# A hybrid decoder step: the bonus term taken out of the token stream, the inversion loading its own matrices, squared keys in another buffer, and the projection jobs in another order

## The chip, the core and the metric

One core of a Trainium2 chip runs the whole step in one launch. The metric is the device time of one execution in microseconds (us), as the median of three runs. Engines are named as in the profile: PE (matmul), DVE (vector), ACT (scalar), POOL (GpSimd), SP (the queue that issues most DMAs).

## The reference, cut to what matters

1024 prompt tokens and 8 x 8 sample tokens (1088 columns) go through one layer. A short convolution makes one half of the mixed vector, an RWKV-7 head group (8 heads of 64) the other; then come the output projection, a squared-ReLU MLP with 4096 hidden features, and the last RMSNorm.

```python
proj = h @ w_in
c_b, c_c, c_x, p_rw = jnp.split(proj, ...)
y_conv = c_b * short_conv(c_c * c_x)
xm = p_rw + (prev - p_rw) * mu
r, k, v, pw, pa, pg = jnp.split(xm, ...)
kk = k * k_k;  kk = kk / max(sqrt(sum(kk * kk)), 1e-12)
k = k * (1 + (a - 1) * k_a)
for t:                      # per head, S is 64 x 64
    S = S * w_t - (S kk_t) (kk_t * a_t)^T + v_t k_t^T
    y_t = S r_t
y = groupnorm(y)
bonus = sum(r * k * r_k, axis=-1, keepdims=True) * v
y_rwkv = (y + bonus) * g
x = x + concat([y_conv, y_rwkv]) @ w_out
x = x + square(relu(rmsnorm(x) @ w_ff1)) @ w_ff2
```

## The kernel before, in words

All matmuls on activations are done in three passes of split 32-bit numbers (high x high, high x low, low x high), 24 matmuls per 128 output features and token group. Tokens stand in three groups of 384, 384 and 320 columns.

**The delta rule in chunks.** The RWKV half is cut into 12 units `UN`: four head pairs p, three token groups g each, so unit u = 3p + g. A unit has six chunks of 64 tokens (five for g = 2, where the fifth holds the sample tokens). For each unit these steps follow each other:

- `gen_norms`: squared keys (ACT, L802), their sums per head (PE `pn`, L806), reciprocals (DVE, L810 to L814).
- `gen_ew`: decays, the modified key `kp`, the products `KB` and `AR`; then the Gram products `pm` (PE, L894), masked by DVE into `LT`, `AMB`, `AMK`. `LT` goes to DRAM and back as blocks of 32 x 32: SP writes `lt_d` (L920) and reads it into `M`, four partition copies inside the tile `gM` (L929). `M` is a single buffer.
- `gen_invert`: POOL inverts the 24 blocks of the unit by 31 pairs of instructions on `W` and `M` (L1024, L1026); SP then writes `w_d` (L1032).
- `gen_merge`: SP reads `Tt` (L1050), PE joins the block inverses (`pz`, L1058 and L1066).
- `gen_tokens`: transposed values `ptv` and keys `ptk` (PE), copied by ACT; after them, in the same stream, the bonus: `kp` times r and r_k (DVE, L969), its split (L973, L976), head sums `pb` (PE, L980), and `bv` (DVE, L986). At L969 the buffers of r and k, and at L986 that of v, are handed back.
- `gen_recur`: the serial recurrence over the chunks (`rc`, L1094 to L1110) and the outputs `py` (L1128); `gen_sample` for the sample chunk; `gen_finish`: GroupNorm (with one power on POOL, L1265), bonus, gate.

**What sets the order.** `Weave.run` takes all these generators, and the stream `fill` of projection matmuls (`acc`, L660), and writes out one fixed order for every engine. Each step names its engine, a planned cost and what must stand before it (`deps`, and credits of buffers in `acq`). A generator is strictly serial: a step that cannot be placed holds all later steps of that generator. On the chip each engine then runs its list in order. There are 24 projection jobs of 72 matmuls in the table `main`, at most two accumulators open. The r, k and v of one p come into three buffers each (`XB`), one per group, so the r projection of the next p needs a buffer that L969 has handed back.

Two waits of the planner matter here. In `gen_ew` the load of `M` for unit u comes as a step of that generator behind the mark `("inv", u - 1)`, the end of the inversion before, and only after it the mark `("A", u)` is set. In `gen_tokens` the bonus of unit u has `deps=[("A", u)]`:

```python
yield ck("SP", 1.6, nb=True, deps=[("inv", u - 1)] if u else [])
M = at["M"]
for i in range(4):
    SP.dma_start(M[24 * i:24 * i + nb], lt_d[:nb])
e["M"] = M
wv.mark(("A", u))
```

Behind the units come the output projection (`out_jobs`, L667), two FF1 jobs inside the weave, and from some 750 us on the MLP, which the change does not touch.

Of the kernel before, what the change touches and what calls it, by code (L numbers as in the profile page):

```python
# [28 lines left out]
REC, TR = 2, 2  # L29
# [4 lines left out]
def tile_kernel(ctx: ExitStack, tc: tile.TileContext, io: dict):  # L34
# [698 lines left out]
    main = (rkv_jobs(0) + conv_jobs(0, "cxb") + conv_jobs(1, "c") + rkv_jobs(1) + conv_jobs(1, "xb") + rkv_jobs(2)  # L733
# [60 lines left out]
    def gen_norms(u):  # L794
# [4 lines left out]
        yield ck("ACT", 0.5, deps=[("xk", p, g)] + ([("pb", u - 1)] if u else []))  # L799
        xk = xs["k", p, g]  # L800
        k2 = at["pe"].tile([128, 384], F32, tag="kx", name="k2")
# [5 lines left out]
        yield ck("DVE", 0.65)  # L807
# [13 lines left out]
    def gen_ew(u):  # L821
# [26 lines left out]
        yield ck("DVE", 0.99, deps=[("xk", p, g)] + ([("pb", u - 2)] if u > 1 else []))  # L848
        xk = xs["k", p, g]
        kp = at["pe"].tile([128, 384], F32, tag="kp", name="kp", bufs=2)  # L850
        e["kp"] = kp
# [74 lines left out]
        yield ck("SP", 1.6, nb=True, deps=[("inv", u - 1)] if u else [])  # L926
        M = at["M"]
        for i in range(4):
            SP.dma_start(M[24 * i:24 * i + nb], lt_d[:nb])  # L929
        e["M"] = M  # L930
        wv.mark(("A", u))
        wv.mark(("M", u), wv.now + 2.3)

    def gen_tokens(u):
# [18 lines left out]
        KT = at["KTs"][u % 2].rearrange("p c (x k) -> p c x k", x=2)  # L953
        for c0 in range(0, nch, 3):
            cc = range(c0, min(c0 + 3, nch))
            yield ck("PE", 0.108 * len(cc), acq=("tr",), deps=[("KB", u)] + done(u - 2))
            KB, kp = e["KB"], e["kp"]
            pt = ps.tile([128, 4, 128], F32, tag="tr", name="ptk", bufs=TR)
            for c in cc:
                PE.transpose(pt[:, c - c0, :], KB[:, c, :], ident)  # L960
            for h in range(2):
                for x in range(2):
                    yield ck("ACT", 0.35, lat=0)
                    A.copy(KT[HS[h], c0:cc[-1] + 1, x, HS[h]], pt[HS[x], 0:len(cc), HS[h]])
            wv.free("tr")
        yield ck("DVE", 0.5, deps=[("A", u)])
        wv.mark(("ptk", u))
        xr, xk = xs.pop(("r", p, g)), xs.pop(("k", p, g))
        V.scalar_tensor_tensor(kp[:, :n], xr[:, :n], vec("rk", p), kp[:, :n], op0=ALU.mult, op1=ALU.mult)  # L969
        wv.free("xr", "xk")  # L970
        yield ck("ACT", 0.42)
        rk_hi = at["pe"].tile([128, 384], F32R, tag="kx", name="rk_hi")
        A.copy(rk_hi[:, :n], kp[:, :n])  # L973
        yield ck("DVE", 0.5)
        rk_lo = at["pe"].tile([128, 384], F32R, tag="rkl", name="rk_lo")
        V.tensor_tensor(rk_lo[:, :n], kp[:, :n], rk_hi[:, :n].bitcast(F32), op=ALU.subtract)  # L976
        wv.mark(("rkr", u))
        yield ck("PE", 0.35, acq=("tr",), deps=[("F", u - 2)] if u > 1 else [])
        pb = ps.tile([128, 512], F32, tag="tr", name="pb", bufs=TR)
        PE.matmul(pb[:, :n], bonesr, rk_hi[:, :n], start=True, stop=False)  # L980
        PE.matmul(pb[:, :n], bonesr, rk_lo[:, :n], start=False, stop=True)
        wv.mark(("pb", u))
        yield ck("DVE", 0.5)
        xs.pop(("v", p, g))
        bv = at["pp"].tile([128, 384], F32, tag="bv", name="bv", bufs=2)
        V.tensor_tensor(bv[:, :n], pb[:, :n], xv[:, :n], op=ALU.mult)  # L986
        wv.free("tr", "xv")
        e.update(KT=KT, VT=VT, bv=bv)
# [13 lines left out]
    def gen_invert(u):  # L1002
# [5 lines left out]
        if u == 0:  # L1008
            yield ck("SP", 0.45)
            load_W(0)  # L1010
        W = Ws.pop(u)
        tmp = at["pp"].tile([96, 80], F32, tag="wtmp", name="wtmp")
        for r in range(31):
            if r == 0:
                yield ck("POOL", 0.63, lat=0, deps=[("M", u), ("W", u)])
                M = e["M"]
# [225 lines left out]
    def gen_finish(u):  # L1242
# [5 lines left out]
        yield ck("DVE", 0.7, deps=[("C", u)] + ([("Y", p)] if g == 2 else []))  # L1248
# [62 lines left out]
    def gen_rows():  # L1311

        for tag, k in ROWS:
            yield ck("ACT", 0.05, lat=0, acq=(tag,), deps=[("T", 10), ("mixd", 6), ("convd", 2, 0)])
            load_row(pa.tile([128, 384], F32, tag=tag, name="mr", bufs=XB[tag[1]]), 0, k)
        yield ck("NO", 0, deps=[("T", 11), ("rows", 0), ("row3", 2)])
# [129 lines left out]
    with tc.manual_schedule():  # L1446
# [13 lines left out]
        for t in range(3):  # L1460
# [6 lines left out]
            if t == 1:  # L1467
# [20 lines left out]
                chain(gen_tokens),  # L1488
# [177 lines left out]
```

## Time and profile before

| what | us |
|---|---|
| median of three runs | 1524.59 (1522.58 to 1525.06) |
| the profiled execution | 1522.59 |
| its span, first to last instruction | 1520.8 |
| PE busy | 1461.6 (96%) |
| DVE busy | 826.0 (54%) |
| POOL busy | 315.4 (21%) |

The page's strip of 40 slices gives the busy share of each engine in tenths, and PEclk the granted TensorE clock in tenths of full speed. A row of the windows view names a stretch, its length, the busy time of PE, PEld, DVE, ACT and POOL with instruction counts, the granted clock and the DMA share. In a timeline row the start, the duration, the engine, the line and the instruction stand, with the idle time before it in brackets. SPq rows are DMA issues.

### The profile page before, as it was taken

How to read it: one execution, taken by the hardware profiler on the slowest of the kernel's cores; microseconds unless marked ns; L12 is line 12 of the kernel's file. 1: busy time of each engine (PE TensorE's matmuls, PEld its weight loads, DVE VectorE, ACT ScalarE, POOL GpSimd, SP SyncE). 2: the span in 40 equal slices, each digit the busy share in tenths (PEclk: the TensorE clock that was granted, in tenths of full speed). 3: DMA queues.
4: the chain of work that ended last, by engine and by line, in shares of the span. 5: the costliest groups of instructions: out<-in, count | busy, mean ns of one | idle time of the engine just before them, and what ended most of it. 6: DMA issues, size and time to landing. Idle time of an engine off the chain costs nothing.

```text
span 1520.8 us, 25883 instructions
## 1 busy us (share of the span) xinstructions
PE 1461.6 (96%) x10163; PEld 1370.2 (90%) x10163; DVE 826.0 (54%) x1788; ACT 510.1 (34%) x1094; POOL 315.4 (21%) x855
## 2 busy tenths in 40 slices
PE   7999989979989998899999999999999999999997
PEld 5999879979978898799999999999999999999996
DVE  7538647956756866476633443434444444444447
ACT  6532234232423323344432222332223322233225
POOL 3022762573664656000000000000000000000004
PEclk9999969989978999699999999999999999999998
DMA  5243212311321241663321111111101111111103
GB/s 186 97 161 92 61 30 71 92 51 45 83 64 42 66 112 24 206 193 111 102 73 42 50 38 39 56 49 49 42 28 56 54 45 42 28 56 56 35 1 118
DMA packets 140228, 108.25 MB, mean 71 GB/s; under 512 B 43837, under 2 KB 131017, under 8 KB 140106
## 3 DMA queue, kind: packets, MB, share of 16 engines
q1 hardware_dynamic: 65322, 61.29, 13.5%
q10 hardware_dynamic: 74784, 45.30, 10.1%
q8 instruction: 80, 1.31, 0.4%
q14 instruction: 42, 0.34, 0.1%
HBM read 88.46 MB, written 18.09 MB: 70 GB/s over the span
## 4 chain that ended last, share of the span: by engine, by line
PE 77%; POOL 9%; DMA 4%; DVE 4%; issue 3%; SPq 1%; ACT 1%; POOLq 0%; ACTq 0%; DVEq 0%
PE acc L103 23%; PE acc L1531 16%; PE acc L660 13%; PE acc L1543 7%; PE acc L667 6%; POOL W L1026 4%; POOL wtmp L1024 4%; DMA wraw<-in_w_out 1%; PE py L1128 1%; PE pm L894 1%; PE pw L512 1%; DMA gM<-lt_d 1%; PE rc L1106 1%; PE rc L1110 1%; PE rc L1098 1%
## 5 line engine op out<-in xcount | busy, mean ns | idle before, releaser
L103 PE MATMUL acc<-h_lo,whi 128*128 128x320 f32 (+1 forms) x720 | 234.8, 326 | 0.0
L103 PE MATMUL acc<-h_hi,wlo 128*128 128x320 f32 (+1 forms) x720 | 234.8, 326 | 0.0
L103 PE MATMUL acc<-h_hi,whi 128*128 128x320 f32 (+1 forms) x720 | 234.7, 326 | 0.0
L660 PE MATMUL acc<-h_lo,whi 128*128 128x384 f32 (+1 forms) x672 | 229.5, 342 | 1.6 <-DVE h_lo L410 1.6
L660 PE MATMUL acc<-h_hi,whi 128*128 128x384 f32 (+1 forms) x672 | 229.7, 342 | 0.4 <-DVE nsT L259 0.3
L660 PE MATMUL acc<-h_hi,wlo 128*128 128x384 f32 (+1 forms) x672 | 229.3, 341 | 0.0
L1533 DVE TENSOR_TENSOR x<-acc,x 128x512 f32<-128x512 f32 (+1 forms) x193 | 132.7, 688 | 125.0 <-PE acc L1531 125.0
L1409 DVE TENSOR_TENSOR slo<-r,shi 128x384 fp32r<-128x384 f32 (+1 forms) x96 | 51.5, 536 | 204.5 <-ACT shi L1407 204.5
L1577 POOL TENSOR_TENSOR rsf<-rsf,nhalf 128x1 f32<-128x1 f32 (+1 forms) x9 | 8.0, 889 | 741.5 <-DVE rsf L1574 740.4
L1024 POOL TENSOR_TENSOR wtmp<-W,gM 96x60 f32<-96x60 f32 (+24 forms) x372 | 122.9, 330 | 160.5 <-DMA gM<-lt_d 83.4
L1531 PE MATMUL acc<-f2h,shi 128*128 128x512 f32 (+1 forms) x386 | 150.2, 389 | 0.0
L1531 PE MATMUL acc<-f2h,slo 128*128 128x512 f32 (+1 forms) x386 | 150.0, 389 | 0.0
L1531 PE MATMUL acc<-f2l,shi 128*128 128x512 f32 (+1 forms) x386 | 149.9, 388 | 0.0
L68 ACT CAST f2h<-f2r 128x1024 fp32r<-128x1024 f32 x32 | 32.0, 1046 | 309.1 <-PE acc L1531 309.1
L103 PEld LDWEIGHTS acc<-h_lo,whi 128*128 128x128 f32 x720 | 135.1, 188 | 0.6
L103 PEld LDWEIGHTS acc<-h_hi,whi 128*128 128x128 f32 x720 | 135.1, 188 | 0.6
L103 PEld LDWEIGHTS acc<-h_hi,wlo 128*128 128x128 f32 x720 | 135.2, 188 | 0.0
L660 PEld LDWEIGHTS acc<-h_lo,whi 128*128 128x128 f32 x672 | 129.1, 192 | 2.9 <-DVE h_lo L410 1.9
L660 PEld LDWEIGHTS acc<-h_hi,whi 128*128 128x128 f32 x672 | 129.4, 193 | 2.0 <-issue 0.4
L1026 POOL TENSOR_TENSOR W<-W,wtmp 96x60 f32<-96x60 f32 (+24 forms) x372 | 124.5, 335 | 29.1
L660 PEld LDWEIGHTS acc<-h_hi,wlo 128*128 128x128 f32 x672 | 129.3, 192 | 1.1
L1403 ACT ACTIVATE r<-acc 128x384 f32<-128x384 f32 (+1 forms) x96 | 45.3, 472 | 150.9 <-PE acc L103 141.2
(308 smaller groups left out, 2894.2 us busy)
## 6 DMA issues: line engine op xcount, KB each, us to landing
f2r<-in_w_ff SPq DMA_DIRECT2D x32, 512.0 KB
wraw<-in_w_ff ACTq DMA_DIRECT2D x64, 256.0 KB
wraw<-in_w_in ACTq DMA_DIRECT2D x48, 256.0 KB
wraw<-in_w_out ACTq DMA_DIRECT2D x48, 256.0 KB
xt<-in_x_prompt SPq DMA_DIRECT2D x8, 512.0 KB
x<-in_x_prompt SPq DMA_DIRECT2D x8, 512.0 KB
out_y_prompt<-out SPq DMA_DIRECT2D x7, 512.0 KB
gM<-lt_d SPq DMA_DIRECT2D x32, 96.0 KB
```

Source lines behind the costliest of these rows:

```text
L68: A.copy(hi, src)
L103: PE.matmul(acc[:, :n], a, b, start=(i == 0), stop=(i == 23))
L512: PE.matmul(pw[:, :n], a, b, start=(i == 0), stop=(i == m - 1))
L660: PE.matmul(acc[:, :n], a, b, start=(k == i == 0), stop=(k == 7 and i == 2))
L667: PE.matmul(acc[:n, :256], a, b, start=(k == i == 0), stop=(k == 7 and i == 2))
L1024: G.tensor_tensor(tv, W[:, 0:nr, r:r + 1].broadcast_to([96, nr, wd]), M[:, r:r + 1, r + 1:32].broadcast_to([96, nr, wd]), op=ALU.mult)
L1026: G.tensor_tensor(W[:, 0:nr, r + 1:32], W[:, 0:nr, r + 1:32], tv, op=ALU.subtract)
L1403: A.activation(r[:, :n], acc[:, :n], AF.Relu)
L1409: V.tensor_tensor(lo, r[:, :n], hi.bitcast(F32), op=ALU.subtract)
L1531: PE.matmul(acc[:, :cn], a, b, start=(j == 0), stop=(j == 3 * FB - 1))
L1533: V.tensor_tensor(x1[t][:, cols], acc[:, :cn], x1[t][:, cols], op=ALU.add)
L1543: PE.matmul(acc[:, :n], a, b, start=(j == 0), stop=(j == 3 * FB - 1))
```

## The change

The bonus becomes a generator of its own, `gen_bonus`. It waits for the mark `("R", u)`, set in `gen_ew` right behind `AR`, and stands ahead of the Gram products in time. It hands r, k and v back itself; v waits for the transposes `("vt", u)`. The squared keys go into the tile `kp` (two buffers) in place of `kx`, so their wait is on the bonus two units back and not one. The four loads of `M` move into `gen_invert`, in front of the first POOL step and behind the `w_d` issue of the unit before; `("A", u)` now stands behind the `lt_d` issue and knows nothing of the inversion. In `gen_tokens` the keys are transposed ahead of the values. The sample state `Sn` gets a wait on the stores of the p before. In `main` the x job of the second convolution block moves ahead of the projections of p = 1. Steps that used to hang on `("T", u)` for the bonus now also name `("bv", u)`.

```diff
-    main = (rkv_jobs(0) + conv_jobs(0, "cxb") + conv_jobs(1, "c") + rkv_jobs(1) + conv_jobs(1, "xb") + rkv_jobs(2)
+    main = (rkv_jobs(0) + conv_jobs(0, "cxb") + conv_jobs(1, "cx") + rkv_jobs(1) + conv_jobs(1, "b") + rkv_jobs(2)
...
-        yield ck("ACT", 0.5, deps=[("xk", p, g)] + ([("pb", u - 1)] if u else []))
+        yield ck("ACT", 0.5, deps=[("xk", p, g)] + ([("pb", u - 2)] if u > 1 else []))
...
-        k2 = at["pe"].tile([128, 384], F32, tag="kx", name="k2")
+        k2 = es[u]["kp"] = at["pe"].tile([128, 384], F32, tag="kp", name="kp", bufs=2)
...
+        wv.mark(("R", u))
...
-        yield ck("SP", 1.6, nb=True, deps=[("inv", u - 1)] if u else [])
-        M = at["M"]
-        for i in range(4):
-            SP.dma_start(M[24 * i:24 * i + nb], lt_d[:nb])
-        e["M"] = M
+        e["lt_d"] = lt_d
         wv.mark(("A", u))
-        wv.mark(("M", u), wv.now + 2.3)
...
+    def gen_bonus(u):
...
+        yield ck("DVE", 0.53, deps=[("R", u)])
+        kp = e["kp"]
+        xr = xs.pop(("r", p, g))
+        xs.pop(("k", p, g))
+        V.scalar_tensor_tensor(kp[:, :n], xr[:, :n], vec("rk", p), kp[:, :n], op0=ALU.mult, op1=ALU.mult)
+        wv.free("xr", "xk")
+        yield ck("ACT", 0.42, deps=[("pb", u - 1)] if u else [])
...
+        PE.matmul(pb[:, :n], bonesr, rk_hi[:, :n], start=True, stop=False)
+        PE.matmul(pb[:, :n], bonesr, rk_lo[:, :n], start=False, stop=True)
+        wv.mark(("pb", u))
+        yield ck("DVE", 0.5)
+        bv = e["bv"] = at["pp"].tile([128, 384], F32, tag="bv", name="bv", bufs=2)
+        V.tensor_tensor(bv[:, :n], pb[:, :n], xs["v", p, g][:, :n], op=ALU.mult)
+        wv.free("tr")
+        wv.mark(("bv", u))
+        yield ck("NO", 0, lat=0, deps=[("vt", u)])
+        xs.pop(("v", p, g))
+        wv.free("xv")
...
+            yield ck("SP", 0.5, nb=True, deps=[("So", p - 1, 4)] if p else [])
             e["Sn"] = Sn = at["pp"].tile([128, NB, 64], F32, tag="Sn", name="Sn")
...
+        yield ck("SP", 1.6, lat=2.3, deps=[("A", u)])
+        M, lt_d = at["M"], e["lt_d"]
+        for i in range(4):
+            SP.dma_start(M[24 * i:24 * i + nb], lt_d[:nb])
+        wv.mark(("M", u), wv.now + 2.3)
...
-                yield ck("POOL", 0.63, lat=0, deps=[("M", u), ("W", u)])
-                M = e["M"]
+                yield ck("POOL", 0.63, lat=0, deps=[("W", u)])
...
-        yield ck("DVE", 0.7, deps=[("C", u)] + ([("Y", p)] if g == 2 else []))
+        yield ck("DVE", 0.7, deps=[("C", u), ("bv", u)] + ([("Y", p)] if g == 2 else []))
...
-                chain(gen_tokens),
+                chain(gen_tokens), chain(gen_bonus),
```

Three places show how the written order moves. On PE, before, the Gram products of unit 3 (`pm` from `AR_1286`, the first of three rotating buffers) stand at the merge of unit 2 (`pz` with ten pieces, the only five-chunk unit so far):

```order
L660 MATMUL acc<-h_lo,whi 128x384
L894 MATMUL pm<-AR_1286,KB 128x128 x8
L1058 MATMUL pz<-wz,LT 32x32 x10
L660 MATMUL acc<-h_hi,wlo 128x384
L660 MATMUL acc<-h_hi,whi 128x384
L660 MATMUL acc<-h_lo,whi 128x384
L660 MATMUL acc<-h_hi,wlo 128x384
L1165 MATMUL pts<-ident,Sn 64x64 x8
L1066 MATMUL pz<-Tt_1284,wz 32x32 x10
```

In the changed kernel the same products stand inside the first chunk of unit 1's recurrence (`rc` with `AR_1287` and `Tt_1285`), a few projection matmuls behind the merge of unit 1:

```order
L1106 MATMUL rc<-VT,KT_1293 128x64
L1107 MATMUL rc<-VT,AMK_1290 128x64
L1110 MATMUL rc<-Gh,AR_1287 128x64
L660 MATMUL acc<-h_hi,wlo 128x384
L660 MATMUL acc<-h_hi,whi 128x384
L660 MATMUL acc<-h_lo,whi 128x384
L660 MATMUL acc<-h_hi,wlo 128x384
L1118 MATMUL rc<-X,Tt_1285 128x64
L660 MATMUL acc<-h_hi,whi 128x384
L660 MATMUL acc<-h_lo,whi 128x384
L895 MATMUL pm<-AR_1286,KB 128x128 x8
L1122 MATMUL rc<-UT,KT_1293 128x64
```

So the Gram products of unit 3 have moved ahead of the merge of unit 2 by a whole unit. On SP, before, the first loads around the inversions of units 0 and 1 (`gM` is the tile that holds `M`):

```order
L999 DMA W<-unit_d 96x256
L920 DMA lt_d<-LT 32x6x32 x4
L929 DMA gM<-lt_d 24x1024 x4
L1032 DMA w_d<-W 192x1x32 x4
L1050 DMA Tt_1284<-w_d 32x6x32 x4
L787 DMA sg<-sig_d 128x384
```

and in the changed kernel at the same place:

```order
L1007 DMA W<-unit_d 96x256
L921 DMA lt_d<-LT 32x6x32 x4
L1044 DMA w_d<-W 192x1x32 x4
L1022 DMA gM<-lt_d 24x1024 x4
L1062 DMA Tt_1284<-w_d 32x6x32 x4
L787 DMA sg<-sig_d 128x384
```

The write of the finished inverse now stands ahead of the next load of `M`. In the changed kernel a second pattern comes with the last unit of each p; this is SP around the end of unit 4 (`lt_d` of unit 5 has five chunks):

```order
L787 DMA sg<-sig_d 128x384
L789 DMA ta<-ta_d 128x384
L1044 DMA w_d<-W 192x1x32 x4
L1062 DMA Tt_1284<-w_d 32x6x32 x4
L921 DMA lt_d<-LT 32x5x32 x4
L1299 DMA mix_d<-gt 128x320
L1022 DMA gM<-lt_d 20x1024 x4
```

Here the write of `LT`, and with it the load of `M`, stands behind both `w_d` and `Tt` of the unit before.

## Rows read from the trace of the kernel before

**Rows 1.** The page's strip of 40 slices of 38 us: three of its lines.
```profile
PE   7999989979989998899999999999999999999997
...
POOL 3022762573664656000000000000000000000004
PEclk9999969989978999699999999999999999999998
```

**Rows 2.** Windows view, one stretch per inversion on POOL: units 0, 3, 4, 7, 8, 11.
```profile
140.75:167.04 26.29, 25.95 (x181) 24.84 (x180) 17.01 (x41) 9.54 (x24) 21.51 (x62) 1.00 0.26 74
...
258.38:286.53 28.15, 27.86 (x237) 25.55 (x236) 26.47 (x69) 9.32 (x22) 23.37 (x63) 1.00 0.25 64
301.42:325.10 23.68, 23.68 (x228) 22.55 (x228) 14.08 (x46) 6.83 (x18) 18.90 (x62) 1.00 0.24 64
...
416.32:440.36 24.04, 20.50 (x167) 17.72 (x166) 16.35 (x48) 5.02 (x12) 19.25 (x62) 0.87 0.26 69
447.76:471.89 24.13, 20.84 (x195) 19.05 (x196) 11.72 (x35) 8.50 (x28) 19.35 (x63) 0.72 0.07 18
...
576.45:603.42 26.97, 24.83 (x209) 23.65 (x207) 17.70 (x43) 12.01 (x32) 22.19 (x63) 1.00 0.08 18
sum 304.86, PE 282.44 PEld 261.98 DVE 204.56 ACT 97.34 POOL 247.49; mean PE 23.54 PEld 21.83 DVE 17.05 ACT 8.11 POOL 20.62
```

**Rows 3.** POOL timeline from the end of unit 2's inversion to the start of unit 3's.
```profile
225.16 0.46 POOL L1026 TENSOR_TENSOR W<-W,wtmp 96x8 f32<-96x8 f32 x1
...
239.70 1.33 POOL L1265 TENSOR_TENSOR va<-va,nhalf 128x6 f32<-128x6 f32 x1 [12.80 <-DVE va L1263]
258.38 0.23 POOL L1024 TENSOR_TENSOR wtmp<-W,gM 96x31 f32<-96x31 f32 x1 [17.35 <-DMA gM<-lt_d]
```

**Rows 4.** Windows view: all inversions together, one slow stretch, and the tail.
```profile
140.75:603.42 462.67, 433.02 (x3904) 400.07 (x3902) 310.75 (x862) 155.94 (x415) 259.00 (x754) 0.92 0.25 64
188.00:222.00 34.00, 28.63 (x209) 24.89 (x208) 12.67 (x44) 11.18 (x34) 20.77 (x72) 0.56 0.13 27
618.00:752.00 134.00, 130.71 (x1125) 127.50 (x1126) 82.41 (x167) 56.15 (x108) 7.31 (x10) 0.92 0.49 152
```

**Rows 5.** SP timeline after the inversion of unit 3 (DMA issues).
```profile
286.55 3.32 SPq L1032 DMA_DIRECT2D w_d<-W  x4
289.97 3.06 SPq L920 DMA_DIRECT2D lt_d<-LT  x4
293.14 1.83 SPq L1050 DMA_DIRECT2D Tt<-w_d  x4
...
295.56 0.74 SPq L929 DMA_DIRECT2D gM<-lt_d  x2
```

**Rows 6.** SP timeline after the inversion of unit 7.
```profile
440.38 3.26 SPq L1032 DMA_DIRECT2D w_d<-W  x4
443.81 1.50 SPq L929 DMA_DIRECT2D gM<-lt_d  x4
```

**Rows 7.** PE timeline: the merge of unit 3 begins.
```profile
298.16 0.41 PE L1058 MATMUL pz<-wz,LT 32*32 32x32 f32 x14
```

**Rows 8.** Unit 0, PE and SP timelines: first Gram product, write of LT.
```profile
124.36 0.38 PE L894 MATMUL pm<-AR,KB 64*128 64x128 f32 x2
...
131.11 3.15 SPq L920 DMA_DIRECT2D lt_d<-LT  x4
```

**Rows 9.** Chain that ended last: 25 projection matmuls in a row.
```profile
125.52 4.48 PE acc L660 x25
```

**Rows 10.** DVE timeline: one step of the bonus, one of the norms.
```profile
142.89 0.61 DVE L969 SCALAR_TENSOR_TENSOR kp<-xr,vecT,kp 128x384 f32<-128x384 f32 x1
...
148.41 0.45 DVE L814 TENSOR_SCALAR nneg<-nsc 64x6 f32<-64x6 f32 x2
```

**Rows 11.** Tile W: POOL's first instruction of each pair, shortest, median and longest.
```profile
L1024 POOL TENSOR_TENSOR wtmp<-W,gM x372: 197/294/865, 140.8 to 602.9; 96x60 f32<-96x60 f32 x18, 96x54 f32<-96x54 f32 x12, 96x66 f32<-96x66 f32 x12, 96x28 f32<-96x28 f32 x12
```

**Rows 12.** Waits of the SP queue, 110 to 690 us: writes of LT behind DVE.
```profile
SPq L920 <- DVE LT L903: 38.1, 7, 12.4
SPq L920 <- DVE LT L900: 33.0, 5, 11.4
```

More of the change, by code (lines that the diff above doesn't have):

```diff
@@ L806, in gen_norms @@
             PE.matmul(pn[64:128, 2 * c:2 * c + 2], k2[:, 64 * c:64 * c + 64], hsel, start=True, stop=True)
-        yield ck("DVE", 0.65)
+        wv.mark(("pn", u))
+        yield ck("DVE", 0.65, deps=done(u - 3))
         nsc = at["pp"].tile([128, 12], F32, tag="nsc", name="nsc", bufs=3)
@@ L847, in gen_ew @@
             A.activation(Eps[:, :, 1:9], b3(cum[:, 256:320]), AF.Exp, scale=-CDEC)
-        yield ck("DVE", 0.99, deps=[("xk", p, g)] + ([("pb", u - 2)] if u > 1 else []))
+        yield ck("DVE", 0.99, deps=[("pn", u)])
         xk = xs["k", p, g]
-        kp = at["pe"].tile([128, 384], F32, tag="kp", name="kp", bufs=2)
-        e["kp"] = kp
+        kp = e["kp"]
         V.tensor_scalar(kp[:, :n], ta[:, :n], kah[:, p:p + 1], okah[:, p:p + 1], op0=ALU.mult, op1=ALU.add)
@@ L937, in gen_tokens @@
         e = es[u]
-        s, n = GROUPS[g]
         nch = NCH[g]
+        KT = at["KTs"][u % 2].rearrange("p c (x k) -> p c x k", x=2)
+        for c0 in range(0, nch, 3):
+            cc = range(c0, min(c0 + 3, nch))
+            yield ck("PE", 0.108 * len(cc), acq=("tr",), deps=[("KB", u)] + done(u - 2))
+            KB = e["KB"]
+            pt = ps.tile([128, 4, 128], F32, tag="tr", name="ptk", bufs=TR)
+            for c in cc:
+                PE.transpose(pt[:, c - c0, :], KB[:, c, :], ident)
+            for h in range(2):
+                for x in range(2):
+                    yield ck("ACT", 0.35, lat=0)
+                    A.copy(KT[HS[h], c0:cc[-1] + 1, x, HS[h]], pt[HS[x], 0:len(cc), HS[h]])
+            wv.free("tr")
+        wv.mark(("ptk", u))
         for c0 in range(0, nch, 3):
@@ L948, in gen_tokens @@
                 PE.transpose(pt[0:64, c - c0, :], xv[:, 64 * c:64 * c + 64], ident)
+            if cc[-1] == nch - 1:
+                wv.mark(("vt", u))
             for h in range(2):
@@ L952, in gen_tokens @@
             wv.free("tr")
[L953 to L988, printed above, removed]
+        e.update(KT=KT, VT=VT)
         if g == 2:
+            yield ck("SP", 0.5, nb=True, deps=[("So", p - 1, 4)] if p else [])
             e["Sn"] = Sn = at["pp"].tile([128, NB, 64], F32, tag="Sn", name="Sn")
@@ L1313, in gen_rows @@
         for tag, k in ROWS:
-            yield ck("ACT", 0.05, lat=0, acq=(tag,), deps=[("T", 10), ("mixd", 6), ("convd", 2, 0)])
+            yield ck("ACT", 0.05, lat=0, acq=(tag,), deps=[("T", 10), ("bv", 10), ("mixd", 6), ("convd", 2, 0)])
             load_row(pa.tile([128, 384], F32, tag=tag, name="mr", bufs=XB[tag[1]]), 0, k)
-        yield ck("NO", 0, deps=[("T", 11), ("rows", 0), ("row3", 2)])
+        yield ck("NO", 0, deps=[("T", 11), ("bv", 11), ("rows", 0), ("row3", 2)])
         pex.close()
@@ L1364, in gen_norm2 @@
     def gen_norm2():
-        yield ck("NO", 0, deps=[("T", 11), ("rows", 0)])
+        yield ck("NO", 0, deps=[("T", 11), ("bv", 11), ("rows", 0)])
         for t in range(6):
```

11 lines of the change are left out of this document (added).

## The prediction, made before the changed kernel had run

> **What bounds the kernel now.** Read the strip of 40 slices first [rows 1]. PE is nearly always busy, so PE looks like the bound; but from 110 to 650 us (slices 3 to 17) its digit drops to 8 and 7 and the granted clock to 6 in the same slices in which POOL is at work, and POOL itself falls to 2 or 3 at regular distances. From 750 us on PE is at 9 throughout, nothing else matters, and the change does not reach there. The gain or loss is made in the 12 units.
>
> Second, one window per inversion [rows 2]. The 12 inversions run one after the other on POOL, from 140.75 to 603.42 us: 462.67 us, of which the sum row gives 304.86 to the inversions (25.4 each). So 157.8 us are the 11 gaps between them. They are of three kinds. Short: unit 7 ends at 440.36 and unit 8 starts at 447.76, 7.4 us. Middle: unit 3 ends at 286.53, unit 4 starts at 301.42, 14.9 us. Long: unit 2 ends at 225.62 (its last instruction starts at 225.16 and takes 0.46), unit 3 starts at 258.38, 32.8 us [rows 3].
>
> Third, the long gap in POOL's timeline [rows 3]: POOL does one GroupNorm power and then waits for the load of `M`. Nothing on POOL or SP is the reason: the Gram products of unit 3 themselves stand late on PE, at the merge of unit 2 (first order fence), and that merge can only run when inversion 2 is done. Why so late? The r projection of p = 1 needs a buffer that the bonus hands back; the bonus waits for `("A", u)`, this for the load of `M`, and this for the end of the inversion before. Projections, bonus and inversion are tied into one loop. Its other face is PE: while POOL inverts, PE has no projection left, and the clock falls with it, for instance to a mean of 0.56 between 188 and 222 us [rows 4], which is mostly the lower of the two levels (1.2 GHz), after stretches of thinly spread recurrence matmuls. Units 6 and 9 open the third and fourth p in the same way as unit 3.
>
> **The change, part by part.** The sum follows the POOL chain, because PE has room: between 140.75 and 603.42 us it was busy 433 us at a mean clock of 0.92 [rows 4]. A mean of 0.92 with levels 0.5 and 1 says that 16%, 74 us, ran at half rate; were they busy like the rest (94%), 69 us, the same work takes 34 us less at full rate: some 399 us.
>
> *Start of the first inversion.* The bonus of unit 0 and the norms of units 1 and 2 now stand ahead of the masks of unit 0 on DVE: three operations of about 0.6 us (the first is the 0.61 row [rows 10]), and two groups of norms, each with the 0.45 row and two smaller operations, an estimated 0.9. That is 3.6 us, with a wait of about 1 for ACT and PE inside the bonus: between 0, if it all fits into idle time, and 8, if PE's Gram products are moved as much again. I take **+5**.
>
> *The inversions.* Nothing in them changes, but DVE works more densely beside them: its 311 us [rows 4] fall into a shorter stretch. In the rows the inversion beside the busiest DVE took longest: 28.15 us with DVE busy 26.5 of them, against 23.68 with 14.1 [rows 2]; and the same POOL instruction takes from 197 to 865 ns [rows 11]. The forecast has DVE at 311 of some 425 us, 73%, where it was 67%. Between 24 and 28 us each I take 26, nearer the middle because the share moves little: **12 x 26 = 312, +7**.
>
> The Trainium skill, "SBUF — State Buffer", section on the two separate sides, says that VectorE and GpSimd hold their common port pair as an exclusive lock, so the later of two instructions blocks fully. By that rule an inversion that always has a busy DVE beside it would always be the long one; the trace agrees for unit 3 (28.15 us) and not for units 4 and 8 (23.68 and 24.13 us), where DVE was busy 59% and 49%.
>
> *The gaps.* The load of `M` goes behind `w_d` on SP. Seven places (after units 0, 1, 2, 5, 6, 8, 9) read `lt_d`, `w_d`, `gM`, as in the second pair of order fences. The gap then is four issues of `w_d` (3.26 us), the issues of `gM`, and the landing; the trace has exactly this after unit 7 [rows 6], and it took 7.4. So 7 x 7.5 = 52.5. Where `gM` stood first the gap had been some 4 us shorter, and that is a loss inside this sum. After unit 3 the order is `w_d`, `lt_d`, `gM`: the pattern that took 14.9 [rows 5] without its `Tt` (1.83 us), so 12.5 to 13; I take 12.5. After units 4, 7 and 10 it is `w_d`, `Tt`, `lt_d`, `gM`, of the same pieces as in [rows 5]: 3 x 14.9 = 44.7. Together **109.7, against 157.8: -48.1**. The three long gaps of 32 us go, because the Gram products of units 3, 6 and 9 now stand a few matmuls behind the merge one unit earlier (first pair of order fences) and are done while POOL still inverts.
>
> Does anything hold them back there? From the end of an inversion to its merge it takes 11.6 us (286.53 to 298.16) [rows 2, 7]. PE then has 4 to 13 us of work up to the Gram products of the unit after next (for unit 3 the order has 12 projection matmuls of 0.18 us [rows 9] and a few small ones in between), and `LT` is on its way 6.75 us after them for unit 0 (124.36 to 131.11 us) [rows 8], perhaps 12 when DVE is busy. With 9 us of work that is 11.6 + 9 + 12 = 32.6 us after an inversion, and the next one ends at 7.5 + 26 = 33.5: it fits, with 1 to 6 us to spare; with 13 it would be 36.6, and the places with 10 to 13 are those written `w_d`, `Tt`, `lt_d`, already counted with 14.9.
>
> *The tail.* Last inversion to end of the output projection: 24 projection matmuls now stand behind the last merge that stood ahead of it, at 4.48/25 = 0.18 us [rows 9], 4.3 us; a dozen output matmuls too, at most 2 us; against it the outputs and bonus of the last units went ahead. Between 0 and 6.5, I take **+3**. PE was busy 130.7 of 134 us in this tail [rows 4], so nothing in it can hide.
>
> *At no cost.* Squared keys in `kp`, keys transposed ahead of values, the wait of `Sn`: the same instructions; what hides them is that ACT was busy only 156 of the 463 us [rows 4]; without that cover a key step would cost some 0.6 us per unit on the way to the Gram products, as the DVE step of that size does [rows 10]. If `Sn` comes late, the queue behind it holds `sg` and `ta` of the next unit; it stands ahead of them by a whole inversion. The x job moved ahead of p = 1 delays that projection by 72 matmuls, 13 us at 0.18 [rows 9], and this is already in the order from which the places above were read.
>
> The sum: 5 + 7 - 48 + 3 = -33. The profiled execution took 1522.6 us, 1.8 more than its span and 2.0 below the median of the runs. **1522.6 - 33 = 1489 us**, the last inversion ending at 140.75 + 5 + 312 + 109.7 = 567 us instead of 603.
>
> PE's 399 us for the same work fit into these 427 us, so PE is close behind POOL, at 93%: of the clock nothing more is added to the sum, since PE's gain is hidden behind POOL's chain.
>
> **The rivals.** *PE becomes the bound, earlier.* If DVE lets the inversions stay at 25.4 and the four wider gaps shrink to 9, the chain is 305 + 52.5 + 36 = 394 us, now below PE's 399; against the 422 us of inversions and gaps in the sum PE's 399 would end 23 us earlier, and the kernel takes 1466. For it: short gaps were seen wherever `M` was ready. Against it: the order itself puts `Tt` between in three places.
>
> *POOL and DVE block each other.* All inversions take 28.15 us [rows 2], 26 us more than in the sum: 1515. This is the lock rule taken to its end; for it speaks every inversion of a dense stretch, against it the small step from 67 to 73%.
>
> *Slower: the SP queue holds the inverse.* In seven places the write of `LT` for the next unit stands on SP ahead of `w_d` of the unit that POOL has just finished. If `LT` comes late, SP waits there, and both the merge and the next inversion wait with it. Before, SP waited for `LT` 12 times, 71.1 us, 5.9 each [rows 12]. If these 5.9 us came on top at all seven places, 41 us: 1530, slower than before. It decides from 33/7 = 4.7 us per place. Against it: in the forecast the Gram products run while POOL inverts, and most of the 71 us were waits with nothing due behind them.
>
> *The loop stays.* The k projection of the next p is late all the same, and three gaps of 32 us remain: no gain on them, 1522. Against it stands the order: these projections are written a unit earlier.
>
> **How the numbers follow.** Forecast 0.50; PE as bound 0.20; POOL and DVE blocking 0.18; loop stays 0.04; SP holding the inverse 0.08. The forecast's own bounds (start 0 to 8, inversion 24.5 to 27, tail 0 to 6.5) are -5 - 18 - 3 and +3 + 12 + 3.5, so 1463 to 1508. With the rival on either side, PE as bound with start and tail at their lower ends (1466 - 8 = 1458) and the blocking one at 1515, the range is 1459 to 1515. It leaves out the last two cases and some of the edges. Measurements of this kernel tell 0.2%, 3 us, from no change. Faster by more: the first three cases, 0.88. Within 0.2%: 0.04. Slower: 0.08.
>
> **What the changed profile would show.** Right: on POOL no gap over 16 us between inversions, seven of about 7.5; the last inversion ends near 567 us; the granted clock stays at or near 1.0 from 190 to 550 us; 750 us onwards looks as before, shifted. Wrong in part: inversions of 28 us throughout, or SP rows of `lt_d` that wait for DVE while POOL stands still. Wrong altogether: gaps of 30 us left on POOL, or a last inversion beyond 600 us.

## The result and the profile after

The changed kernel takes 1489.89 us (median of four runs, 1488.44 to 1490.12) against 1523.83 for the kernel before in the same comparison: ratio 0.9775, 95% interval 0.9758 to 0.9792. The forecast was 1489.0. The profiled execution took 1490.12 us; its span is 1488.4 us, 32.4 less than before. In the changed kernel POOL's first instruction of a pair is L1036 (before L1024), the issue of `w_d` L1044, of `lt_d` L921, the load of `M` L1022, of `Tt` L1062.

The strip of 40 slices of the changed kernel, 37 us each, against [rows 1]:

```profile
PE   6999999999999989899999999999999999999997
...
POOL 4021666556656642000000000000000000000004
PEclk9999999999999999999999999999999999999999
```

The clock digit is 9 throughout, and POOL keeps 5 or 6 where it used to fall to 2 and 3. The windows view of the changed kernel, for all inversions with their gaps and for the place of the slow stretch (columns as in [rows 4]):

```profile
145.40:565.39 419.99, 400.13 (x3925) 369.87 (x3924) 299.09 (x836) 149.15 (x404) 255.79 (x754) 0.97 0.27 70
190.00:222.00 32.00, 32.00 (x320) 29.84 (x320) 23.60 (x69) 13.91 (x38) 19.98 (x58) 1.00 0.31 76
```

PE was busy 400 of these 420 us, and in the second stretch, where the mean clock had been 0.56, it never paused and had the upper level of 2.4 GHz throughout. POOL's timeline at the place of the old 32.8 us gap, end of unit 2 to start of unit 3, answers to [rows 3]:

```profile
238.08 0.21 POOL L1038 TENSOR_TENSOR W<-W,wtmp 96x8 f32<-96x8 f32 x1
238.24 1.34 POOL L1277 TENSOR_TENSOR va<-va,nhalf 128x6 f32<-128x6 f32 x1
246.50 0.23 POOL L1036 TENSOR_TENSOR wtmp<-W,gM 96x31 f32<-96x31 f32 x1 [6.92 <-DMA Tt<-w_d]
```

Between 238.29 and 246.50 us stand 8.2 us. The table reads POOL's timeline of every run in this way: inversions are the times from the first to the last instruction of each of the 12, gaps what lies between them, the tail what is left of the span after the last one.

| kernel | ratio (95%) | first starts | inversions | gaps (longest) | tail | span |
|---|---|---|---|---|---|---|
| before | 1 | 140.8 | 304.9 | 157.8 (32.8) | 917.4 | 1520.8 |
| changed | 0.9775 (0.9758-0.9792) | 145.7 | 302.1 | 117.5 (16.7) | 923.0 | 1488.4 |
| e_mload_alone | 1.0040 (1.0026-1.0053) | 139.7 | 303.0 | 175.3 (38.2) | 909.0 | 1527.0 |
| e_order_alone | 0.9927 (0.9907-0.9947) | 139.0 | 306.5 | 147.3 (31.3) | 917.1 | 1509.9 |
| e_mload_back | 0.9827 (0.9807-0.9847) | 146.2 | 299.5 | 123.4 (18.1) | 922.9 | 1492.0 |
| e_order_back | 1.0363 (1.0326-1.0399) | 144.6 | 300.7 | 240.7 (56.3) | 895.0 | 1581.0 |
| e_order_pn | 0.9795 (0.9778-0.9811) | 146.4 | 302.3 | 117.0 (21.8) | 920.6 | 1486.3 |
| e_after_pn | 0.9768 (0.9754-0.9783) | 146.0 | 297.9 | 127.9 (22.6) | 915.7 | 1487.5 |
| e_bonus_pn | 0.9827 (0.9811-0.9844) | 146.8 | 301.4 | 126.4 (19.3) | 920.5 | 1495.1 |
| e_k2_back | 1.0422 (1.0395-1.0449) | 146.1 | 291.9 | 225.0 (63.2) | 925.1 | 1588.0 |
| e_k2_fin | 0.9884 (0.9860-0.9909) | 146.4 | 313.3 | 142.5 (23.1) | 898.3 | 1500.5 |
| e_pool_long | 1.0014 (0.9998-1.0031) | 145.5 | 335.8 | 115.4 (16.5) | 924.9 | 1521.6 |
| e_pool_short | 0.9592 (0.9571-0.9614) | 143.7 | 234.8 | 153.0 (22.0) | 928.2 | 1459.7 |
| e_half_m | 0.9739 (0.9712-0.9766) | 144.3 | 300.3 | 114.2 (17.9) | 922.8 | 1481.5 |

The gaps of the changed kernel, in order, are 8.6, 7.6, 8.2, 12.9, 14.8, 7.6, 8.9, 14.2, 7.7, 10.3 and 16.7 us: the three kinds that the order fences announced. A short gap on its SP timeline, after unit 1, whose last POOL instruction ends at 205.32 us:

```profile
205.35 3.26 SPq L1044 DMA_DIRECT2D w_d<-W  x4
208.78 1.51 SPq L1022 DMA_DIRECT2D gM<-lt_d  x4
210.45 1.77 SPq L1062 DMA_DIRECT2D Tt<-w_d  x4
...
489.21 4.30 SPq L1044 DMA_DIRECT2D w_d<-W  x4
493.61 0.46 SPq L1151 DMA_DIRECT2D out_new_wkv_p<-AMB  x1
494.21 1.54 SPq L1022 DMA_DIRECT2D gM<-lt_d  x4
```

After unit 1 the next inversion starts at 212.96: 3.3 us of `w_d` issues, 1.5 of `gM` issues, and 2.7 from the last issue to the start. The three rows below stand after unit 9: there the issues of `w_d` took 4.3, and a store stands in between, so the gap was 10.3. A wide one, after unit 4, whose inversion ends at 308.44 us:

```profile
308.46 3.33 SPq L1044 DMA_DIRECT2D w_d<-W  x4
313.23 1.78 SPq L1062 DMA_DIRECT2D Tt<-w_d  x4
315.06 2.71 SPq L921 DMA_DIRECT2D lt_d<-LT  x4
...
319.00 1.41 SPq L1022 DMA_DIRECT2D gM<-lt_d  x4
```

The pattern is the one of [rows 5]. `LT` was late as well: on DVE its last masked piece was started 4.3 us after the inversion had ended.

```profile
312.75 0.29 DVE L901 SCALAR_TENSOR_TENSOR LT<-pm,nsc,smask 64x64 f32<-64x64 f32 x1
```

It was done at 313.04 us, 2.0 us before its write was issued at 315.06. So the queue, with `Tt` in front, set this gap, but a write ahead of `Tt` could have gone at most those 2 us earlier.

### The profile page after: what moved, and what is told of

Same layout as the page of the kernel before. It is cut to its first block, busy times and chain, and to the rows that moved or that the text cites. A ratio compares the mean times of both kernels' runs of the same rounds, so it can differ in the third digit from the quotient of the medians.

```text
span 1488.4 us, 25865 instructions
## 1 busy us (share of the span) xinstructions
PE 1436.3 (97%) x10163; PEld 1346.4 (90%) x10163; DVE 823.0 (55%) x1788; ACT 508.9 (34%) x1094; POOL 312.0 (21%) x855
## 3 DMA queue, kind: packets, MB, share of 16 engines
q10 hardware_dynamic: 74784, 45.30, 10.4%
## 4 chain that ended last, share of the span: by engine, by line
PE 66%; POOL 16%; DMA 6%; issue 4%; DVE 3%; SPq 3%; ACT 1%; ACTq 0%; POOLq 0%; DVEq 0%
PE acc L103 24%; PE acc L1543 17%; PE acc L660 9%; POOL W L1038 8%; PE acc L1555 8%; POOL wtmp L1036 8%; PE acc L667 5%; DMA mr<-mix_d 2%; DMA gM<-lt_d 1%; SPq L1044 1%; PE pw L512 1%; SPq L1022 1%; DMA lt_d<-LT 1%; PE pt L399 1%; DVE out L1602 0%
## 5 line engine op out<-in xcount | busy, mean ns | idle before, releaser
L103 PE MATMUL acc<-h_hi,whi 128*128 128x320 f32 (+1 forms) x720 | 234.8, 326 | 0.0
L1036 POOL TENSOR_TENSOR wtmp<-W,gM 96x60 f32<-96x60 f32 (+24 forms) x372 | 119.0, 320 | 164.8 <-DMA gM<-lt_d 58.7
```

The costliest lines, as they stand in the source:

```text
L103: PE.matmul(acc[:, :n], a, b, start=(i == 0), stop=(i == 23))
L1036: G.tensor_tensor(tv, W[:, 0:nr, r:r + 1].broadcast_to([96, nr, wd]), M[:, r:r + 1, r + 1:32].broadcast_to([96, nr, wd]), op=ALU.mult)
```

## The experiments

**Which part carries the gain.** First the loads of `M` alone, moved in the kernel before, and then put back in the changed one:

```diff
-        yield ck("SP", 1.6, nb=True, deps=[("inv", u - 1)] if u else [])
-        M = at["M"]
...
+        yield ck("SP", 1.6, lat=2.3, deps=[("A", u)])
+        M, lt_d = at["M"], e["lt_d"]
...
```

The lines with a minus stand in `gen_ew`, those with a plus in `gen_invert`; for e_mload_back the diff runs the other way.

> The kernel before with one part of the change: the four loads of M stand in the inversion's stream, behind the write of the finished inverse; the bonus stays in the token stream, the job order stays. Theory (the loop): the Gram products of units 3, 6 and 9 still stand at the merge of the unit before, so the three long gaps of 32 us on POOL stay, and the short gaps of 3.6 us grow to 7.5: 1523 to 1540 us. Rival (the gain comes from the M load no longer tied to the element-wise stream): most of the gain, 1490 to 1500 us.

Measured 1528.73 us (ratio 1.0040). The long gaps stay at 38, 32 and 29 us and the short ones that had been 3.6 to 4.3 become 7.5 to 8.5: by itself this part is a small loss. One link of the loop in the prediction is gone in this kernel: `("A", u)`, and with it the bonus, no longer waits for the inversion before, and the bonus of unit 2 starts on DVE at 209.0 us, where it had been 215.3. That the long gaps stay all the same points at something else that holds the Gram products; it is shown below, after the squared keys.

> The changed kernel with the loads of M back in the element-wise stream and its wait on the inversion before; bonus stream, buffer of the squared keys and job order as changed. Theory (the loop): the written order keeps the Gram products a unit early, so no gap of 30 us on POOL; 1480 to 1497 us, the faster end if short gaps fall to 3.6 us. Rival (the M load is the part that matters): 1515 to 1525 us, long gaps back.

Measured 1495.42 us. This is inside the theory's range: beside the other parts the moved loads are worth 5.5 us (1495.4 - 1489.9), no more.

Then the table of jobs alone, and put back:

```diff
-    main = (rkv_jobs(0) + conv_jobs(0, "cxb") + conv_jobs(1, "c") + rkv_jobs(1) + conv_jobs(1, "xb") + rkv_jobs(2)
+    main = (rkv_jobs(0) + conv_jobs(0, "cxb") + conv_jobs(1, "cx") + rkv_jobs(1) + conv_jobs(1, "b") + rkv_jobs(2)
```

> The kernel before with the new order of projection jobs alone. Theory (the loop): bonus and M load still tie the projections to the inversion, three to four long gaps on POOL stay: 1515 to 1530 us. Rival (the job order alone feeds PE): 1490 to 1505 us.

Measured 1512.2 us, 0.7% faster, between the two ranges: three long gaps (31, 29, 31 us) stay, as the theory said, and the other eight shrink together from 60.6 to 56.0 us.

> The changed kernel with the old order of projection jobs. Theory (the loop): the written order now puts the Gram products of units 4, 7 and 9 at or near the merge of the unit before, so two or three gaps of 25 us and more come back on POOL: 1510 to 1535 us. Rival (the job order is a detail, the bonus alone opens the loop): 1485 to 1497 us.

Measured 1578.55 us: both expectations missed it. The changed kernel without its new table is 3.6% slower than before. POOL stood still for 56.3 us between units 2 and 3. The PE timeline of e_order_back shows where the Gram products of unit 3 were:

```profile
251.47 1.16 PE L895 MATMUL pm<-AR,KB 64*128 64x128 f32 x16
...
268.82 0.74 PE L806 MATMUL pn<-bonesr,kp 128*64 128x2 f32 x10
...
300.75 0.76 PE L895 MATMUL pm<-AR,KB 64*128 64x128 f32 x8
```

and its DVE timeline what stood just ahead of the second half:

```profile
300.29 0.17 DVE L811 TENSOR_SCALAR nsc<-pn 64x10 f32<-64x10 f32 x1
```

The Gram products were cut in two, 49 us apart, and between them stands `pn`, the norms of unit 5, written at 268.82 and read by DVE only at 300.29. One line of the change explains this, and the prediction had not spoken of it: the reciprocals now wait for the end of the recurrence three units back, with their PSUM buffer already taken.

```diff
         yield ck("PE", 0.117 * nch + 0.1, gap=0.1, acq=("tr",))
         ...
-        yield ck("DVE", 0.65)
+        wv.mark(("pn", u))
+        yield ck("DVE", 0.65, deps=done(u - 3))
```

There are two buffers `tr`, and a half of the Gram products needs both. If `pn` holds one for 31 us, they cannot be placed.

**The held buffer, tested.** In three kernels that wait was put ahead of `pn`, where nothing is held yet:

```diff
-        yield ck("PE", 0.117 * nch + 0.1, gap=0.1, acq=("tr",))
+        yield ck("PE", 0.117 * nch + 0.1, gap=0.1, acq=("tr",), deps=done(u - 3))
...
-        yield ck("DVE", 0.65, deps=done(u - 3))
+        yield ck("DVE", 0.65)
```

> The changed kernel with the old job order, as in e_order_back, but the norms' wait for the end of the recurrence three units back (done(u - 3), which the change put on their DVE step) now stands on their PE step, ahead of pn. Theory: in e_order_back pn of unit 5 took one of the two PSUM buffers tr and kept it until the recurrence of unit 2 had ended, and the second half of the Gram products, which need both buffers, stood behind it (251 and 301 us on PE in unit 3). With pn behind that wait the buffer is held for about 2 us: no gap over 20 us between inversions, total 1488 to 1508 us. Rival (the old job order itself starves PE, since the r projection of the next p comes up too early for its buffer): the gap of 56 us stays in the main, total 1560 to 1585.

Measured 1491.97 us: 87 us gone by moving one wait. The windows view over the same stretch, first of e_order_back:

```profile
226.00:330.00 104.00, 80.98 (x708) 74.46 (x706) 64.33 (x167) 26.71 (x70) 39.09 (x111) 0.86 0.22 59
```

and of e_order_pn:

```profile
226.00:330.00 104.00, 99.12 (x1018) 90.32 (x1019) 83.97 (x234) 38.49 (x105) 60.40 (x176) 1.00 0.29 76
```

In the same 104 us PE did 1018 instead of 708 matmuls. One gap of 21.8 us is a little over the 20 of the expectation.

> The changed kernel, its job order kept, with the norms' wait on their PE step as in e_order_pn. Theory: in the new job order pn never holds its PSUM buffer for long while Gram products wait, so little changes: 1483 to 1496 us, gaps as in the changed kernel within 3 us each but for a few places. Rival (the hold still costs in the wider gaps of 12.9 to 16.7 us): those five gaps fall to about 8, sum of gaps near 95, total 1465 to 1475.

Measured 1486.72 us, inside the theory's range and some 3 us better than the changed kernel, too little to tell from it (the intervals of the two ratios overlap). The gaps fit less well: four of the eleven differ by more than 3 us from those of the changed kernel, the longest is 22.6, and together they are 10.4 us longer, while the tail is 7.3 us shorter. With the wait moved, the new table of jobs is worth some 5 us (1486.72 against 1491.97, with ratio intervals that just overlap). So in the change it mainly moves the written order past the place where the held buffer would hurt.

> The bonus stream and the squared keys in kp alone: old job order, the loads of M back in gen_ew, and the norms' wait on their PE step. Theory: once no PSUM buffer is held across a wait, the bonus stream carries nearly the whole gain by itself: 1490 to 1510 us, no gap over 22 us. Rival (job order or the move of the M loads is needed for it): gaps of 30 us or more between the p, total over 1515.

Measured 1496.39 us: the bonus stream with the squared keys in `kp`, with neither the new table nor the moved loads, brings 26.6 of the 34 us, and no gap is over 19.3. The moved loads add 4.4 us on top (against 1491.97); e_mload_back had 5.5. The keys transposed ahead of the values, the wait of `Sn` and the norms' new wait stand in this kernel too, as in every one built on the changed kernel; no run takes them out.

**The squared keys.** The prediction had them at no cost.

```diff
-        yield ck("ACT", 0.5, deps=[("xk", p, g)] + ([("pb", u - 2)] if u > 1 else []))
+        yield ck("ACT", 0.5, deps=[("xk", p, g)] + ([("pb", u - 1)] if u else []))
...
-        k2 = es[u]["kp"] = at["pe"].tile([128, 384], F32, tag="kp", name="kp", bufs=2)
+        k2 = at["pe"].tile([128, 384], F32, tag="kx", name="k2")
...
```

In the part left out `gen_ew` takes the buffer `kp` again itself, behind the bonus two units back, as it did before the change.

> The changed kernel with the squared keys back in the one-buffer tile that the bonus also uses, and their wait on the bonus of the unit before. Theory (the loop): the written order then puts the Gram products of units 3, 6 and 9 behind the merge of the unit before, three long gaps come back: 1510 to 1535 us. Rival (this buffer is a detail): 1486 to 1497 us.

Measured 1587.93 us: the direction was right, the loss of 98 us is three times the middle of the range. Gaps of 45, 49 and 63 us stand ahead of units 3, 6 and 9. The PE timeline of e_k2_back around the first gap names a chain:

```profile
245.59 0.84 PE L1289 MATMUL pty<-ident,yn 128*128 128x128 f32 x3
...
248.78 0.31 PE L949 MATMUL pb<-rk_hi,bonesr 128*128 128x320 f32 x1
...
250.10 0.86 PE L806 MATMUL pn<-bonesr,k 128*64 128x2 f32 x12
```

and its POOL timeline the start of it:

```profile
237.98 0.21 POOL L1038 TENSOR_TENSOR W<-W,wtmp 96x8 f32<-96x8 f32 x1
238.14 1.34 POOL L1277 TENSOR_TENSOR va<-va,nhalf 128x6 f32<-128x6 f32 x1
```

The norms of unit 3 (`pn`) wait for the bonus of unit 2 (`pb`), which needs a buffer `bv` (there are two) from the finish of unit 0 (`pty`), and that waits for its GroupNorm power, which stands on POOL behind the whole inversion of unit 2. So unit 3 cannot begin its own way to POOL before POOL has finished unit 2. To test this, the planner was allowed to put the power ahead of an inversion's waiting steps:

```diff
-                chain(gen_invert),
+                chain(gen_finish), chain(gen_invert),
...
-                chain(gen_finish), chain(gen_sample, range(2, 12, 3)),
+                chain(gen_sample, range(2, 12, 3)),
```

The place in this list decides where two steps could start at the same time, so the edit can also settle such ties on the other engines.

> e_k2_back (squared keys again in the one buffer kx, so the norms of unit u wait for pb of unit u - 1), with one edit: the planner may place the GroupNorm power of gen_finish on POOL ahead of the waiting steps of an inversion, no longer behind all 31 pairs. Theory: in e_k2_back the norms of unit 3 wait for pb of unit 2, pb (two buffers bv) for the finish of unit 0, and that finish for its power, which stands on POOL behind the whole inversion of unit 2 (pty of unit 0 at 245.59, pb at 248.78, pn at 250.10 us on PE). With the power inside the inversion, at 1.3 us each, the gap after unit 2 falls from 49 (third long gap 63) to under 25 us, total 1498 to 1530 us. Rival (the single kx buffer alone makes the norms late, whatever POOL does): the three gaps stay at 40 us or more, total over 1560.

Measured 1503.69 us, 84 us less, and the gap after unit 2 is 16.0 us. In the PE timeline of e_k2_fin the same three stand some 22 us earlier:

```profile
223.94 0.55 PE L1289 MATMUL pty<-ident,yn 128*128 128x128 f32 x3
...
226.02 0.39 PE L949 MATMUL pb<-rk_hi,bonesr 128*128 128x320 f32 x1
...
227.46 0.86 PE L806 MATMUL pn<-bonesr,k 128*64 128x2 f32 x12
```

since on its POOL timeline the power now runs inside the inversion:

```profile
220.73 0.27 POOL L1038 TENSOR_TENSOR W<-W,wtmp 96x50 f32<-96x50 f32 x1
220.96 1.34 POOL L1277 TENSOR_TENSOR va<-va,nhalf 128x6 f32<-128x6 f32 x1
```

The price is in the table: inversions of 313.3 us together. What `kp` does in the change is to cut this chain at another place, since the norms then wait for the bonus two units back.

**The same chain in the kernel before.** There, too, the norms wait for the bonus of the unit before. These rows of its POOL, DVE, PE and ACT timelines, those of the chain alone and in order of time, begin where the inversion of unit 2 ends:

```profile
225.57 1.33 POOL L1265 TENSOR_TENSOR va<-va,nhalf 128x6 f32<-128x6 f32 x1
226.41 0.55 DVE L877 TENSOR_TENSOR AR<-xr,Ep 128x384 f32<-128x384 f32 x1
...
232.90 0.49 PE L1277 MATMUL pty<-ident,yn 128*128 128x128 f32 x3
...
235.56 0.42 PE L980 MATMUL pb<-rk_hi,bonesr 128*128 128x320 f32 x1
236.01 0.62 ACT L802 ACTIVATE k<-xk,vecT 128x384 f32<-128x384 f32 x1 [2.98 <-PE pb L980]
237.12 0.86 PE L806 MATMUL pn<-bonesr,k 128*64 128x2 f32 x12
...
239.15 1.16 PE L894 MATMUL pm<-AR,KB 64*128 64x128 f32 x16
```

`AR` of unit 3 was done at 227.0 us. Its Gram products started 12.2 us later, at 239.15, because its squared keys had to wait for `pb` of unit 2, this for the finish of unit 0, and this for the GroupNorm power behind the inversion of unit 2. Ahead of units 6 and 9 the same steps follow each other: the power at 353.62 and 471.84, the squared keys at 363.37 and 481.18, the Gram products at 367.80 and 484.99. In e_mload_alone they stand at 230.50, 243.13 and 251.58 for unit 3: the same chain runs through its gap. In the changed kernel the squared keys of unit 3 run at 201.49 and its Gram products at 221.36. No run breaks only this chain in the kernel before.

**What bounds the changed kernel.** POOL's chain was made longer and shorter at an unchanged written order:

```diff
+            for _ in range(2 if r < 8 else 1):
+                G.tensor_tensor(tv, W[:, 0:nr, r:r + 1].broadcast_to([96, nr, wd]),
...
```

> The changed kernel, same written order on every engine, with eight POOL instructions more in each inversion (the first of a pair done twice in the first eight steps, same result): 8 x 0.33 = 2.6 us per unit, 31 us in all. Theory (POOL's chain sets the end of the units): 25 to 35 us over the changed kernel, 1515 to 1525 us. Rival (PE is the bound, POOL has slack): 1489 to 1496 us.

Measured 1524.54 us: inversions 33.7 us longer, span 33.2 us longer, gaps unchanged. POOL's chain sets the end one for one.

For e_pool_short it is, in the same loop over r (this kernel leaves out the end of each inversion, so its inverses are incomplete and its results wrong):

```diff
+            if r >= 23:
+                continue
```

> The changed kernel, same written order, with the last eight of the 31 steps of each inversion left out (5 to 6.7 us per unit, some 65 us in all). Theory: POOL's chain gets shorter until PE's own work (399 us from the first inversion on) and the path from merge to the next Gram products hold it: 20 to 35 us less, 1455 to 1470 us. Rival (POOL alone counts): 60 us less or more, under 1435 us. Rival (PE is already the bound): 1484 to 1490 us.

Measured 1461.53 us. The inversions fell by 67.3 us but the gaps grew by 35.5, so the span fell by 28.7 only. The windows view of e_pool_short from the first to the last inversion says why:

```profile
143.70:531.52 387.82, 383.65 (x3818) 356.05 (x3817) 294.32 (x826) 148.15 (x401) 203.41 (x562) 0.99 0.29 76
```

PE is busy 383.65 of 387.82 us at a clock of 0.99. So PE is the next bound, some 30 us below the changed kernel; this is read from its busy share, and no run made PE's own work longer or shorter. The window holds 3818 matmuls; for the 3925 of the changed kernel's window this rate would give an estimated 394 us.

**The loads of `M` in two halves.** `M` is loaded in two halves, so that the first half can stand ahead of `w_d` and is free as soon as the inversion before has passed its 16th step:

```diff
+    def gen_mhalf(u, x):
+        nb = 4 * NCH[UN[u][1]]
+        yield ck("SP", 1.6, deps=[("A", u)] + ([(("invh", "inv")[x], u - 1)] if u else []))
+        M, lt_d = at["M"], es[u]["lt_d"]
+        for i in range(4):
+            SP.dma_start(M[24 * i:24 * i + nb, 16 * x:16 * x + 16], lt_d[:nb, 16 * x:16 * x + 16])
+        wv.mark(("M", u, x), wv.now + 2.3)
...
```

In `gen_invert`, not shown here, the first step waits for the first half and the 17th for the second.

> The changed kernel with M loaded in two halves: the first 16 rows as soon as POOL has done step 15 of the inversion before and LT is written, the other 16 when it has ended. Theory (gaps on POOL count one for one until PE binds): where LT is early, gaps of 7.5 us fall to 2 to 4; where LT is late, nothing; 8 to 25 us less than the changed kernel, 1465 to 1482 us. Rival (PE or the path from merge to Gram products already sets the pace): 1486 to 1495 us.

Measured 1483.39 us (ratio 0.9739), between the two expectations, 1.4 us above the theory's range. It is the lowest time of a kernel that computes the whole reference, but the intervals of the two ratios overlap, so a gain over the changed kernel is not shown. On its POOL timeline unit 1 follows unit 0 after 1.0 us:

```profile
170.72 0.21 POOL L1043 TENSOR_TENSOR W<-W,wtmp 96x8 f32<-96x8 f32 x1
171.98 0.24 POOL L1041 TENSOR_TENSOR wtmp<-W,gM 96x31 f32<-96x31 f32 x1 [1.06 <-DMA gM<-lt_d]
```

and on its SP timeline the eight loads stand ahead of `w_d`:

```profile
167.87 4.31 SPq L1016 DMA_DIRECT2D gM<-lt_d  x8
172.27 3.37 SPq L1051 DMA_DIRECT2D w_d<-W  x4
```

Only two of the eleven gaps become this short (1.0 and 1.2); the others are 8.6 to 17.9 us, and the sum falls by 3.3 us only. After unit 1, for one, `w_d` was issued first and `lt_d` behind it.

## Why the prediction was right

By its own terms, from the table:

| term | forecast | measured |
|---|---|---|
| start of the first inversion | +5 | +5.0 (140.75 to 145.72) |
| inversions | +7 | -2.8 (304.9 to 302.1) |
| gaps | -48.1 | -40.3 (157.8 to 117.5) |
| tail | +3 | +5.6 (917.4 to 923.0) |
| sum | -33 | -32.4 |

*Right.* The long gaps go: none is over 16.7 us (the text said 16). The last inversion ends at 565.39 us (said 567), and the clock is 1.00 where it was 0.56, and 0.97 on the mean from 190 to 550 us. The start fits to a tenth, and so does its cause: with bonus and norms ahead of it, the first Gram product of unit 0 moved from 124.36 [rows 8] to 128.59 us. The gap after unit 3 is 12.9 (said 12.5), the three behind `Tt` and `lt_d` 45.7 together (said 44.7).

*Two sizes were off and cancelled.* The inversions missed by 9.8 us and the gaps by 7.8 the other way; that the sum fits to 1 us is luck. The gaps had been given no bounds of their own in the range. The inversions were to grow to 26 us and are 25.2: DVE was busy 299 of 420 us, 71%, where 73% had been forecast, and nothing got longer. By this trace a denser DVE did not lengthen the inversions, so the rival of 28.15 us throughout falls. The prediction took it from the lock rule for any busy DVE. The Trainium skill ("SBUF — State Buffer", section "SBUF: two separate sides") limits that lock to VectorE instructions in a two-port mode or with two SBUF inputs, and no run here tells these instructions apart. [rows 11] mixes shapes; for one shape, 96x60, the first instruction of a pair took 0.29 to 0.85 us in the kernel before. The seven short gaps were to be 7.5 each, 52.5 us; they are 7.6 to 10.3, 58.9. The one row they were taken from, 7.4 us [rows 6], was shorter than all seven: after unit 9 the issues of `w_d` took 4.3 us and a store stood in between, and after units 0, 6 and 9 the time from the last issue of `gM` to POOL's start was 3.5 to 3.8 us, where it was 2.7 after unit 1.

*Wrong: what made the long gaps.* The prediction named one tie, the r projection behind the bonus, `("A", u)` and the load of `M`, and said that nothing on POOL was the reason. The runs show a second tie that ended later, and it begins on POOL: GroupNorm power, finish, bonus, squared keys, norms. e_mload_alone takes the wait for the inversion out of the named loop, and three gaps of 29 to 38 us stay. e_k2_back has the bonus stream and gives the norms their old wait back, and they are 45 to 63 us. The named tie is real as well: with the bonus in its own stream the keys of unit 3 were there at 201.5 us, before at 219.4. So the bonus stream does not give the gain without the `kp` edit, which the prediction had as a detail; that the same change also broke the second tie was luck as far as the argument goes.

*The tail.* It came out near the upper bound. The windows view of the changed kernel, as far behind the last inversion as the third stretch of [rows 4]:

```profile
580.00:714.00 134.00, 123.84 (x1015) 119.83 (x1014) 80.64 (x164) 53.02 (x103) 4.47 (x7) 0.96 0.51 160
```

and three pieces of its chain that ended last (start, us, what):

```profile
596.98 7.05 DMA mr<-mix_d
614.77 9.00 DMA mr<-mix_d
627.60 7.07 DMA mr<-mix_d
```

PE stood still for 10 of 134 us, where it had been 3.3 [rows 4]: the last pieces of the mixed vector reach the output projection by way of DRAM, and the chain runs through these loads. The added work is there as counted: behind the last merge stand 24 more projection matmuls and 12 more output matmuls than before. What the idle time adds to it is not separated: that PE had other work to cover the loads before, and has less now, is a reading of the two windows, and no run tested it.

*PE as the bound.* PE's own work had been put at 399 us. It was busy 400 in the changed kernel; at the rate of e_pool_short the same number of matmuls takes an estimated 394, so this rival was a few us further away than the text had it. e_pool_long shows POOL as the bound.

*SP holding the inverse.* The waits of the SP queue of the changed kernel, 110 to 650 us:

```profile
SPq L1044 <- POOL W L1038: 98.4, 12, 25.2
...
SPq L921 <- DVE LT L904: 56.2, 7, 11.9
```

SP still waits for `LT`, 56.2 us in this row, but `w_d` itself waits 12 times for POOL: the queue had come round before the inversion ended. The rival needed 4.7 us more at each of seven places and got 0.9 ((58.9 - 52.5)/7).

*What it had missed.* "At no cost: squared keys in `kp`" was right about the price and blind to what hangs on it: without that edit the same bonus stream costs 98 us (1587.93 against 1489.89). And the new wait of the norms, which holds a PSUM buffer, was not priced at all; the new table of jobs keeps it harmless, and without that table it costs 89 us. The forecast got past both only because it was read from the written order of the changed kernel, in which both are already settled. As the cause of the gain, it named the loop through the bonus; e_bonus_pn shows that the bonus stream and `kp` together give 26.6 of the 34 us, and the moved loads give 4.4 to 5.5. The bonus stream without `kp` was run only with everything else changed (e_k2_back), and `kp` without the bonus stream was not run; no run isolates the remaining few us.

## What to carry to other kernels

Where a planner writes the order, read the places of the late steps from that order and price the gaps by the queue's rows: that was good to within 10 us per term. But the order does not say which wait put a step where it is: here `AR` had been ready for 12 us, and the step that ended last stood behind a small power on POOL. One edit of such a kernel is not worth what it shows alone: parts that gain nothing or lose by themselves can be the condition for the others, and an ablation must be read in the trace as well. A step that takes a scarce buffer should have all its waits ahead of the taking; one wait behind it turned a gain of 31 us (e_order_pn) into a loss of 56 (e_order_back).

## What the runs showed that had not been expected

Most of a short gap between two inversions is issue on one queue: four issues of `w_d`, which the next inversion does not need, take 3.3 us, four of `gM` 1.5, and 2.7 us pass from the last issue to POOL's start, 7.6 us in all. Where e_half_m has its loads ahead of `w_d` the gap is 1.0 us.

Taking 67.3 us from the bounding engine gave 28.7 back: with PE busy 99% (383.65 of 387.82 us) about half of the freed time turned into gaps, 35.5 us, at an unchanged order of the program.
